# Gated delta net and forgetting attention block: mask and scaling products moved to ScalarE, fp32r low parts from GpSimd to VectorE, output transposes one step later

## The chip, the cores and the metric

The kernel runs on one core of one Trainium2 chip (trn2). The metric is device time in microseconds (us) of one execution, the median of several runs. Engines are named as the profile names them: PE (TensorE matmul), PEld (its weight loads), DVE (VectorE), ACT (ScalarE), POOL (GpSimd), SP (SyncE, which issues most DMAs).

## The reference, cut to what matters

One layer on 1024 tokens of width 1024: input LayerNorm, one input projection, a gated delta net with 4 heads of 128 and forgetting attention with 8 heads of 64, output projection, LayerNorm, squared-ReLU MLP with a gated embedding, LayerNorm. The two parts that the change touches:

```python
# gated delta net, chunks of 64
kk = jnp.einsum('bhnid,bhnjd->bhnij', k, k)
a_mat = jnp.where(strict, kk * beta[..., :, None] * decay, 0.0) + jnp.eye(CHUNK, dtype=f32)
sol = lax.linalg.triangular_solve(a_mat, rhs, left_side=True, lower=True, unit_diagonal=True)
k_dec = k * jnp.exp(gam[..., -1:] - gam)[..., None]
# forgetting attention, blocks of 128 queries
s = s + c_i[..., :, None] - c_all[..., None, :]
attn = jax.nn.softmax(s, axis=-1)
return jnp.einsum('bhqk,bkhd->bqhd', attn.astype(v.dtype), v)
```

## The kernel before, in words

Products in full precision are made of three fp32r matmuls: each operand x is stored as a rounded high part `hi` and a low part `lo = x - hi`, and hi*hi, hi*lo and lo*hi are added up in PSUM. The helper `split_lo(eng, lo, src, hi)` (line 53; its instruction has line L54) makes the low part on the engine that it is given. Another helper, `tt` (L48), is a product, sum or difference of two tensors; `stt` (L51) has a row factor as well. A tile framework orders the instructions of each engine: it follows the program and its priorities, and puts work of low priority where it expects an engine to wait. Each engine then works through its own list in order, and so does each DMA queue.

The stages in order of time: embeddings, LayerNorm and values; the q, k, v columns of the delta net (`conv_silu`, PE tile `g`, three PSUM banks in turn: ACT scales a finished bank into `cv`, DVE adds three shifted products of the bank and takes its last three columns as `edge`, which frees it); then the delta net of heads 0 and 1 (`gdn_a(0)`, `gdn_fs(0)`, `gdn_b(0)`, `gdn_chain(0)`), of heads 2 and 3 (the same with 1), and forgetting attention; after it the output projection (PE tile `ps_mix`), the gate and the MLP, which the change leaves as they are. Projections with low priority (further `g` tiles, then `fq` and `fk` for the attention's q and k, then `gz` for the delta net's gate) fill PE in between.

`gdn_a` computes for each head and each pair of chunks a 128x128 product of keys (PE tile `ps_aq`); DVE scales and masks it into `ka[:, 1]` (line 543, shown as L51). That array goes to DRAM (`img`, lines 549 and 571), from where the 32x32 diagonal blocks come back as `fa`. Lines 550 to 555 multiply `ka[:, 1]` by the mask `m32` into `am` and by `m64` in place, and the keys `kd` by a row factor, six DVE products of 128x1024. `gdn_fs` inverts the diagonal blocks by forward substitution, 62 small DVE instructions (`ftmp`, `ft`), and sends the result through DRAM into `tm` (SP queue) and `ttm` (ACT queue), on which `gdn_b` then works (PE tiles `ps_p`, `ps_tp`, `ps_ttp`).

In attention, `fox_start(h)` loads a head's q and k (`qkr`), casts them to `qa` and `ka` and makes the low parts `qa[64:128]` and `kl`; every second head also loads values (`vr`) and makes `va`. Of the 64 steps (head, block of queries), `fox_a` makes the scores (`ps_sc`), adds the decay with a row minimum on DVE (`s,m`, L758) and takes the exponential on ACT; `fox_b` transposes it (`ps_pt`, two PSUM banks) into `pth` and `ptl`, with POOL writing zeros (`pth<-zero`, `ptl<-zero`); `fox_c` multiplies by the values (`ps_av`), copies that to `ot` on ACT, transposes it (`ps_oq`) and reduces it into `osb`. `fox_pair` normalises a pair of heads (`fsq`, `fss`, `nwt`, `fn`, and a product over `osb`); `fox_out` transposes a pair's outputs into `act_hi` and `act_lo`. `gdn_mix(h)` brings a delta net head into the same arrays: it loads `o` and, from `z_spill`, the gate `szl`, transposes `o` into a bank that it shares with `ps_pt`, and multiplies on DVE. `load_half` loads and splits the output weights (`wo_raw`, `wo`).

In attention POOL makes `ka`, `kl`, the low parts of `va`, of `gdn_mix` and of `wo`, and the last product over `osb`. `o`, `qkr` and `vr` share the two buffers of tag `qk_raw`; `szl` and the `sz` of the gate projection share the three buffers of tag `cv`.

Of the kernel before, what the change touches and what calls it, by code (L numbers as in the profile page):

```python
# [8 lines left out]
F32 = mybir.dt.float32  # L9
# [6 lines left out]
P = 128  # L16
# [6 lines left out]
DH = 64  # L23
# [14 lines left out]
def tile_block(ctx: ExitStack, tc: tile.TileContext, x, p, ln_in_g, ln_in_b, w_in, conv_w, a_log, dt_bias,  # L38
# [432 lines left out]
    nc.vector.memset(m32, 0.0)
    nc.vector.memset(m32[0:32, 32:64], 1.0)
    nc.vector.memset(m32[64:96, 96:128], 1.0)
    nc.vector.memset(m64, 0.0)
    nc.vector.memset(m64[0:64, 64:128], 1.0)
    H = {}

    def gdn_a(hp):
# [68 lines left out]
        for j, h in enumerate(hs):  # L547
            c = H[h]
            nc.sync.dma_start(out=img_full(0, h), in_=c["ka"][:, 1])
            tt(nc.vector, c["am"], c["ka"][:, 1], m32.unsqueeze(1).to_broadcast([P, 8, P]), ALU.mult)  # L550
        for j, h in enumerate(hs):
            c = H[h]
            tt(nc.vector, c["ka"][:, 1], c["ka"][:, 1], m64.unsqueeze(1).to_broadcast([P, 8, P]), ALU.mult)
            tt(nc.vector, c["kd"], c["kd"], cc[:, 1, 8 * j:8 * j + 8].unsqueeze(2).to_broadcast([P, 8, P]), ALU.mult)
        for half in range(2):
# [154 lines left out]
    def fox_load(h):  # L710
        pr, j = h // 2, h % 2
        raw = [fp.tile([P, T], F32, tag="qk_raw", name=f"qkr{h}_{w}", bufs=2) for w in range(2)]
        for w in range(2):
            for half in range(2):
                nc.sync.dma_start(out=raw[w][_sl(half, 64)], in_=qk_spill[w, pr, _sl(j, 64), :])
        qa = fh[j].tile([P, T], F32R, tag="qa", name=f"qa{h}")
        ka = fh[j].tile([P, T], F32R, tag="ka", name=f"ka{h}")
        kl = fh[j].tile([P, T], F32R, tag="kl", name=f"kl{h}")
        nc.scalar.copy(out=qa, in_=raw[0])
        split_lo(nc.vector, qa[64:128], raw[0][64:128], qa[64:128])  # L720
        nc.gpsimd.tensor_copy(out=ka, in_=raw[1])
        split_lo(nc.gpsimd, kl, raw[1], ka)
        cb = fh[j].tile([P, T], F32, tag="cb", name=f"cb{h}")
        nc.sync.dma_start(out=cb, in_=row_spill[32 + h * 8:40 + h * 8, :].rearrange("c i -> (c i)").partition_broadcast(P))
        return qa, ka, kl, cb

    def fox_values(pr):
        raw = fp.tile([P, 8, 2, DH], F32, tag="qk_raw", name=f"vr{pr}", bufs=2)
        nc.sync.dma_start(out=raw.rearrange("q t a d -> q t (a d)"),
                          in_=v_spill[:, _sl(pr)].rearrange("(t q) c -> q t c", q=P))  # L730
        va = []
        for j in range(2):
            va.append(fvp.tile([P, 8, 2, DH], F32R, tag="va", name=f"va{pr}_{j}", bufs=3))
            nc.scalar.copy(out=va[j][:, :, 0], in_=raw[:, :, j])
            split_lo(nc.gpsimd, va[j][:, :, 1], raw[:, :, j], va[j][:, :, 0])
        return va
# [51 lines left out]
    def fox_c(h, g):  # L788

        j = h % 2  # L790
        nk = 2 * g + 2
        va, osb, _ = pairs[h // 2]
        pth, ptl = tiles.pop((h, "c", g))
        po = psf.tile([P, 512], F32, tag="av", name="ps_av", bufs=1)
        for kb in range(nk):
            for i, pt in enumerate((pth, ptl)):
                nc.tensor.matmul(po[:, 0:256], va[j][:, kb].rearrange("q a d -> q (a d)"),  # L797
                                 pt[:, kb].rearrange("q a b -> q (a b)"),
                                 start=(kb == 0 and i == 0), stop=(kb == nk - 1 and i == 1))
        ot = fr.tile([P, 256], F32, tag="ot", name="ot")  # L800
        nc.scalar.copy(out=ot, in_=po[:, 0:256])
        pq = psf.tile([P, 512], F32, tag="av", name="ps_oq", bufs=1)
        for i in range(2):
# [4 lines left out]
    def fox_pair(pr):  # L808
# [14 lines left out]
        tt(nc.vector, fn, fn, lsf, ALU.mult)  # L823
        tt(nc.gpsimd, o16, o16, fn.unsqueeze(2).to_broadcast([P, 16, DH]), ALU.mult)

# [22 lines left out]
    def gdn_mix(h):  # L848
# [3 lines left out]
        for half in range(2):  # L852
            s = cp.tile([P, 512], F32, tag="cv", name="szl", bufs=3)
            nc.sync.dma_start(out=s, in_=z_spill[h, :, _sl(half, 512)])
            ps = psf.tile([P, 512], F32, tag="pt", name="ps_ot")
            for i in range(4):
                nc.tensor.transpose(ps[:, _sl(i)], o[:, half * 4 + i], ident)
            stt(s, ps, gdn_gh, s, ALU.mult, ALU.mult)
            hi = act_hi[half][:, :, h]
            s = s.rearrange("q (t i) -> q t i", i=P)  # L860
            nc.scalar.copy(out=hi, in_=s)
            split_lo(nc.gpsimd, act_lo[half][:, :, h], s, hi)

# [7 lines left out]
    for i in range(n + 12):  # L871
# [63 lines left out]
    def load_half(w, n, tiles, name):  # L935
        out = []
        for k2 in range(NK // 2):
# [534 lines left out]
```

## Time and profile before

| | |
|---|---|
| median of 3 runs | 1447.7 us (1447.67 to 1448.51) |
| the profiled execution, its own time | 1447.75 us |
| its span from first to last instruction | 1446.0 us |
| PE busy | 1387.1 us, 96% |
| DVE busy | 1091.0 us, 75% |
| ACT busy | 553.1 us, 38% |
| POOL busy | 102.6 us, 7% |
| mean granted TensorE clock | 0.992 |

A busy share is a mean over stages. Waits are read from the idle time that a row shows in square brackets, with what ended it; a matmul's own length is longer than the step from its start to the next start, since matmuls are pipelined.

### The profile page before, as it was taken

To read this page: it belongs to the slowest core of one execution; us is meant where nothing else is said; L and a number is where in the kernel's file an instruction comes from. 1 tells how busy PE (TensorE), PEld (TensorE's weight loads), DVE (VectorE), ACT (ScalarE), POOL (GpSimd) and SP (SyncE) were. 2 spreads that over 40 slices of the span, in tenths; PEclk is the share of its full clock that TensorE was granted. 3 is DMA by queue.
4 is the path that set the end of the run, shared out by engine and by line. 5 is a ranking of instruction groups with operands and counts; after the bars stand their busy time and mean duration, and the time that the engine had idled before them with its cause. 6 is when DMAs were issued, how large, how long until landed. Compare 5 with 4: busy or idle time off the path is not lost.

```text
span 1446.0 us, 20592 instructions
## 1 busy us (share of the span) xinstructions
PE 1387.1 (96%) x7342; PEld 1167.7 (81%) x7342; DVE 1091.0 (75%) x2290; ACT 553.1 (38%) x1016; POOL 102.6 (7%) x128
## 2 busy tenths in 40 slices
PE   7999989999999999699999999999999999999997
PEld 5988868988887777578889988888888888888885
DVE  6758899689378886657899776667777689757877
ACT  5223423241247765651124333233333444455421
POOL 1000000000024332440000000000000000000000
PEclk9999999999999999899999999999999999999999
DMA  9856435444553433432476764444444985334342
GB/s 303 252 167 208 124 92 134 130 162 125 146 156 88 124 97 114 131 124 88 153 267 199 214 215 147 139 145 159 155 160 164 310 302 185 96 101 131 110 139 80
DMA packets 195869, 229.10 MB, mean 158 GB/s; under 512 B 23877, under 2 KB 128566, under 8 KB 195766
## 3 DMA queue, kind: packets, MB, share of 16 engines
q1 hardware_dynamic: 186374, 221.48, 48.8%
q10 hardware_dynamic: 9008, 5.24, 1.4%
q8 instruction: 58, 0.95, 0.3%
q0 software_dynamic: 384, 1.06, 0.2%
q14 instruction: 45, 0.37, 0.1%
HBM read 152.14 MB, written 75.60 MB: 157 GB/s over the span
## 4 chain that ended last, share of the span: by engine, by line
PE 78%; DVE 9%; DMA 7%; issue 3%; ACT 2%; POOL 1%; SPq 0%; DVEq 0%; ACTq 0%; POOLq 0%
PE ps_uP L1204 21%; PE ps_da L1324 9%; PE ps_db L1324 9%; PE g L218 6%; PE ps_gP L1071 5%; PE ps_db L1430 3%; PE fk L218 3%; PE ps_mix L950 3%; PE psv L320 3%; PE ps_av L797 2%; PE fq L218 2%; PE gz L218 2%; PE ps_pt L783 2%; DVE h L51 2%; DVE cv L51 1%
## 5 line engine op out<-in xcount | busy, mean ns | idle before, releaser
L1204 PE MATMUL ps_uP<-T,uS 128*128 128x512 f32 x576 | 133.8, 390 | 0.0
L1204 PEld LDWEIGHTS ps_uP<-T,uS 128*128 128x128 f32 x576 | 108.0, 188 | 23.5 <-ACT ua L1209 0.2
L1294 ACT CAST rh<-rr 128x512 fp32r<-128x512 f32 x112 | 69.8, 623 | 141.5 <-PE ps_db L1324 47.9
L54 DVE TENSOR_TENSOR rl<-rr,rh 128x512 fp32r<-128x512 f32 x112 | 77.1, 690 | 57.0 <-ACT rh L1294 28.9
L1204 PE MATMUL ps_uP<-B,uA 128*128 128x512 f32 x384 | 92.2, 395 | 0.0
L950 PE MATMUL ps_mix<-wo,act_hi 128*128 128x512 f32 x256 | 83.0, 399 | 3.5 <-POOL wo L54 1.7
L1204 PEld LDWEIGHTS ps_uP<-B,uA 128*128 128x128 f32 x384 | 72.0, 188 | 17.3
L218 PE MATMUL g<-act_hi,in_hi 128*128 128x512 f32 x192 | 76.4, 398 | 5.0 <-DVE edge L431 5.0
L218 PE MATMUL g<-act_hi,in_lo 128*128 128x512 f32 x192 | 75.9, 397 | 0.6 <-DVE in_lo L54 0.6
L218 PE MATMUL g<-act_lo,in_hi 128*128 128x512 f32 x192 | 75.8, 395 | 0.0
L1294 ACT CAST rl<-B 128x512 fp32r<-128x512 f32 x96 | 59.5, 621 | 22.5 <-PE ps_db L1324 12.4
L54 DVE TENSOR_TENSOR uA<-uraw,uA 128x512 fp32r<-128x512 f32 x48 | 33.2, 692 | 46.0 <-ACT uA L1199 46.0
L1199 ACT CAST uS<-wS 128x512 fp32r<-128x512 f32 x64 | 39.4, 621 | 73.2 <-issue 48.2
L54 DVE TENSOR_TENSOR ql<-B,rl 128x512 fp32r<-128x512 f32 x96 | 65.9, 687 | 0.5 <-ACT rl L1294 0.2
L950 PEld LDWEIGHTS ps_mix<-wo,act_hi 128*128 128x128 f32 x256 | 47.5, 188 | 14.1 <-POOL wo L54 2.4
L783 PE MATMUL ps_pt<-ident,s 128*128 128x128 f32 x288 | 45.3, 277 | 14.1 <-DVE szl L51 8.9
L54 DVE TENSOR_TENSOR ptl<-ps_pt,pth 128x512 fp32r<-128x512 f32 (+2 forms) x96 | 50.9, 552 | 8.0 <-ACT pth L785 7.4
L761 ACT ACTIVATE s<-s,m 128x128 f32<-128x128 f32 (+3 forms) x64 | 50.0, 781 | 14.9 <-DVE m L758 11.4
L51 DVE SCALAR_TENSOR_TENSOR cv<-g,hcw,cv 128x510 f32<-128x510 f32 (+2 forms) x72 | 53.4, 741 | 1.0 <-ACT cv L424 0.5
L1324 PE MATMUL ps_db<-rl,rh 128*128 128x512 f32 x192 | 51.3, 389 | 0.0
L1324 PE MATMUL ps_db<-ql,rh 128*128 128x512 f32 x192 | 51.3, 389 | 0.0
L1324 PE MATMUL ps_db<-rl 128*128 128x512 f32 x192 | 51.3, 389 | 0.0
(369 smaller groups left out, 3675.5 us busy)
## 6 DMA issues: line engine op xcount, KB each, us to landing
uraw<-in_w_up_dram SPq DMA_DIRECT2D x32, 512.0 KB, 4.2
B<-in_w_down_dram SPq DMA_DIRECT2D x32, 512.0 KB, 5.9
rr<-rS SPq DMA_DIRECT2D x64, 256.0 KB, 2.7
in_raw<-in_w_in_dram SPq DMA_DIRECT2D x24, 512.0 KB, 4.3
rr<-rA SPq DMA_DIRECT2D x48, 256.0 KB, 2.9
h_spill<-h SPq DMA_DIRECT2D x16, 512.0 KB, 4.0
qkr<-qk_spill SPq DMA_DIRECT2D x32, 256.0 KB, 4.4
rA<-ub SPq DMA_DIRECT2D x32, 256.0 KB, 2.2
```

What stands on the lines that cost most here:

```text
L51: nc.vector.scalar_tensor_tensor(out=o, in0=a, scalar=s, in1=b, op0=op0, op1=op1)
L54: eng.tensor_tensor(out=lo, in0=src, in1=hi.bitcast(F32), op=ALU.subtract)
L218: mm = nc.tensor.matmul(ps, w[:, k, :], a[n][:, :, k], start=(k == 0 and wi == 0), stop=(k == NK - 1 and wi == 2))
L320: nc.tensor.matmul(ps[:, 0:264], a[t // 4][:, t % 4, k], w[:, k, _sl(n, 264)], start=(k == 0 and wi == 0), stop=(k == NK - 1 and wi == 2))
L761: nc.scalar.activation(out=s[:, :W], in_=s[:, :W], func=AF.Exp, bias=m[:, i:i + 1], scale=-1.0, accum_out=pairs[h // 2][2][:, r, j:j + 1])
L783: nc.tensor.transpose(pt[:, i], s[:, _sl(k0 + i)], ident)
L950: nc.tensor.matmul(ps, a[t // 4][:, t % 4, k], w, start=(k == 0 and wi == 0), stop=(k == NK - 1 and wi == 2))
L1071: nc.tensor.matmul(ps[j // 2][:, j % 2], B[b][s][k][:, _sl(j)], a[w][:, k], start=(first and j % 2 == 0 and k == 0 and wi == 0), stop=(j % ...
L1204: nc.tensor.matmul(ps[p], w[:, k], B[t][b][k], start=(chain is None and k == 0 and wi == 0), stop=(k == 3 and wi == 2), skip_group_check=c ...
L1294: nc.scalar.copy(out=hi, in_=src)
L1324: nc.tensor.matmul(ps[j], rs[x][:, _sl(j)], qs[y], start=(not chain and c == 0 and wi == 0), stop=(c == NP - 1 and wi == 2), skip_group_ch ...
L1430: nc.tensor.matmul(b[j], rs[x][:, i, _sl(j - js[0])], Q[c0 + i][y], start=(c0 == 0 and i == 0 and wi == 0), stop=(c0 + i == NP - 1 and wi ...
```

## The change

In `gdn_a`, the mask products become copies on ACT with a factor per row (0 or 1, from the small table `mrow`) for the column blocks that are kept, and DVE `memset`s for the blocks that are zero; the product on `kd` becomes 16 ACT copies of 128x128 (eight for each head) with the factor of the row. In attention, the cast `ka` goes from POOL to ACT, and the low parts `kl`, `va`, those of `gdn_mix` and of `wo`, and the product over `osb` from POOL to DVE; POOL keeps the zeros. The transposes and the sum of an output block leave `fox_c` and become `fox_d`, one step later. The gate `szl` takes its buffers from tag `th` instead of `cv`.

```diff
-    m32 = gp.tile([P, P], F32, name="m32")
-    m64 = gp.tile([P, P], F32, name="m64")
...
+    mrow = gp.tile([P, 3], F32, name="mrow")
+    nc.vector.memset(mrow, 0.0)
+    for i, (r0, r1) in enumerate(((0, 32), (64, 96), (0, 64))):
+        nc.vector.memset(mrow[r0:r1, i:i + 1], 1.0)
...
             nc.sync.dma_start(out=img_full(0, h), in_=c["ka"][:, 1])
-            tt(nc.vector, c["am"], c["ka"][:, 1], m32.unsqueeze(1).to_broadcast([P, 8, P]), ALU.mult)
+
+            for b0, i in ((32, 0), (96, 1)):
+                nc.scalar.activation(out=c["am"][:, :, b0:b0 + 32], in_=c["ka"][:, 1, :, b0:b0 + 32], func=AF.Copy,
+                                     scale=mrow[:, i:i + 1])
+            nc.vector.memset(c["am"].rearrange("q c (b i) -> q c b i", i=32)[:, :, 0:3:2], 0.0)
         for j, h in enumerate(hs):
             c = H[h]
-            tt(nc.vector, c["ka"][:, 1], c["ka"][:, 1], m64.unsqueeze(1).to_broadcast([P, 8, P]), ALU.mult)
-            tt(nc.vector, c["kd"], c["kd"], cc[:, 1, 8 * j:8 * j + 8].unsqueeze(2).to_broadcast([P, 8, P]), ALU.mult)
+            nc.scalar.activation(out=c["ka"][:, 1, :, 64:128], in_=c["ka"][:, 1, :, 64:128], func=AF.Copy,
+                                 scale=mrow[:, 2:3])
+            nc.vector.memset(c["ka"][:, 1, :, 0:64], 0.0)
+            for ch in range(8):
+                nc.scalar.activation(out=c["kd"][:, ch], in_=c["kd"][:, ch], func=AF.Copy,
+                                     scale=cc[:, 1, 8 * j + ch:8 * j + ch + 1])
...
-        nc.gpsimd.tensor_copy(out=ka, in_=raw[1])
-        split_lo(nc.gpsimd, kl, raw[1], ka)
+        nc.scalar.copy(out=ka, in_=raw[1])
+        split_lo(nc.vector, kl, raw[1], ka)
...
-            split_lo(nc.gpsimd, va[j][:, :, 1], raw[:, :, j], va[j][:, :, 0])
+            split_lo(nc.vector, va[j][:, :, 1], raw[:, :, j], va[j][:, :, 0])
...
-        ot = fr.tile([P, 256], F32, tag="ot", name="ot")
+        ot = tiles[h, "o", g] = fr.tile([P, 256], F32, tag="ot", name="ot")
         nc.scalar.copy(out=ot, in_=po[:, 0:256])
+
+    def fox_d(h, g):
+
+        j, osb, ot = h % 2, pairs[h // 2][1], tiles.pop((h, "o", g))
         pq = psf.tile([P, 512], F32, tag="av", name="ps_oq", bufs=1)
...
-        tt(nc.gpsimd, o16, o16, fn.unsqueeze(2).to_broadcast([P, 16, DH]), ALU.mult)
+        tt(nc.vector, o16, o16, fn.unsqueeze(2).to_broadcast([P, 16, DH]), ALU.mult)
...
-            s = cp.tile([P, 512], F32, tag="cv", name="szl", bufs=3)
+            s = cp.tile([P, 512], F32, tag="th", name="szl", bufs=3)
...
-            split_lo(nc.gpsimd, act_lo[half][:, :, h], s, hi)
+            split_lo(nc.vector, act_lo[half][:, :, h], s, hi)
...
+        if 3 <= i < n + 3:
+            h, r = steps[i - 3]
+            if r % 2:
+                fox_d(h, r // 2)
                 if r == 7 and h % 2:
                     fox_pair(h // 2)
-                    later[max(i + 8, n - 14 + 4 * (h // 2))] = h // 2
+                    later[max(i + 7, n - 14 + 4 * (h // 2))] = h // 2
...
-            split_lo(nc.gpsimd, lo, raw, hi)
+            split_lo(nc.vector, lo, raw, hi)
```

The framework places everything around these edits anew. Three places follow; a number behind a name tells one buffer from another.

First DVE in `gdn_a(0)`, from the first product behind the last `ps_aq` scaling on (`g_1997` and `g_2032` are two projection tiles that follow each other; `vb` are the values). Before:

```order
L48 TENSOR_TENSOR am_1693<-ka_1696,m_1217 128x1024
L48 TENSOR_TENSOR am_1695<-ka_1710,m_1217 128x1024
L48 TENSOR_TENSOR kd_1698<-kd_1698,cc_1794 128x1024
L48 TENSOR_TENSOR ka_1696<-ka_1696,m_1218 128x1024
L48 TENSOR_TENSOR ka_1710<-ka_1710,m_1218 128x1024
L48 TENSOR_TENSOR kd_1712<-kd_1712,cc_1794 128x1024
L48 TENSOR_TENSOR vb_1697<-ps_vt,cc_1794 128x512
...
L48 TENSOR_TENSOR ftmp<-fa_1885,ft_1886 64x31
L51 SCALAR_TENSOR_TENSOR cv<-g_1997,hcw,cv 128x511
...
L431 COPY edge<-g_1997 128x3
```

Now (the tiles are `g_2015` and `g_2050`, and the 511 columns of `g_2015` stand ahead of the `ps_aq` scalings):

```order
L48 TENSOR_TENSOR vb_1695<-ps_vt,cc_1792 128x512
...
L557 MEMSET ka_1694 128x8x64
L51 SCALAR_TENSOR_TENSOR cv<-g_2015,hcw,cv 128x510
L51 SCALAR_TENSOR_TENSOR cv<-g_2050,hcw,cv 128x511
L557 MEMSET ka_1708 128x8x64
L51 SCALAR_TENSOR_TENSOR cv<-g_2015,hcw,cv 128x509
L431 COPY edge<-g_2015 128x3
...
L48 TENSOR_TENSOR ftmp<-fa_1903,ft_1904 64x31
```

Six products left the list, two memsets entered it, and `edge` now stands ahead of the forward substitution instead of behind its first steps.

Second DVE at the end of `gdn_fs(0)`; `fa<-ft` is the copy behind its last step. Before, with `g_2348` the last but two of the `g` tiles (`g_2392` and `g_2427` follow):

```order
L48 TENSOR_TENSOR ftmp<-fa_1885,ft_1886 64x31
L51 SCALAR_TENSOR_TENSOR cv<-th,cv 128x512
L48 TENSOR_TENSOR ft_1886<-ft_1886,ftmp 64x31
L51 SCALAR_TENSOR_TENSOR cv<-g_2348,hcw,cv 128x511
L579 COPY fa_1885<-ft_1886 64x1024
```

Now, with `g_2445` the very last of them:

```order
L48 TENSOR_TENSOR ftmp<-fa_1903,ft_1904 64x31
L51 SCALAR_TENSOR_TENSOR cv<-g_2445,hcw,cv 128x511
L48 TENSOR_TENSOR ft_1904<-ft_1904,ftmp 64x31
L51 SCALAR_TENSOR_TENSOR cv<-edge,hcw,cv 128x1
L585 COPY fa_1903<-ft_1904 64x1024
```

The last step of the substitution moved from ahead of the products on `g_2348` to behind the first product on the last `g` tile. On PE, 24 `fq` matmuls stand between that last `g` tile and the first `ps_p` before, and 47 now.

Third the SP queue in heads 6 and 7 of the attention (`o`, `qkr` and `szl` as above). Before:

```order
L851 DMA o_6021<-o_spill 128x1024
L458 DMA z_spill<-sz 128x512
L724 DMA cb_6090<-row_spill 128x1024
L715 DMA qkr_0_6077<-qk_spill 64x1024 x2
L940 DMA wo_raw<-in_w_out_dram 128x2x512
L715 DMA qkr_1_6078<-qk_spill 64x1024 x2
L458 DMA z_spill<-sz 128x512 x2
L851 DMA o_6248<-o_spill 128x1024
L854 DMA szl<-z_spill 128x512 x2
```

Now:

```order
L861 DMA o_6059<-o_spill 128x1024
L458 DMA z_spill<-sz 128x512
L730 DMA cb_6124<-row_spill 128x1024
L721 DMA qkr_0_6111<-qk_spill 64x1024 x2
L864 DMA szl<-z_spill 128x512 x2
L721 DMA qkr_1_6112<-qk_spill 64x1024 x2
L864 DMA szl<-z_spill 128x512 x2
L954 DMA wo_raw<-in_w_out_dram 128x2x512
L861 DMA o_6286<-o_spill 128x1024
```

Before, the first `szl` stands behind the third `o` (`o_6248`); now three `szl` have gone out still earlier, among the loads of the first heads, and the next four stand ahead of that `o` (`o_6286`).

## Rows read from the trace of the kernel before

**Rows 1.** The page's chain that ended last: shares of the span by engine.

```profile
PE 78%; DVE 9%; DMA 7%; issue 3%; ACT 2%; POOL 1%; SPq 0%; DVEq 0%; ACTq 0%; POOLq 0%
```

**Rows 2.** Windows: stretch, its length, each engine's busy us and count, granted clock, DMA share, GB/s.

```profile
420.00:650.00 230.00, 208.13 (x1286) 169.52 (x1285) 168.53 (x449) 142.59 (x322) 91.61 (x106) 0.98 0.39 117
506.50:529.00 22.50, 21.39 (x143) 17.73 (x142) 19.58 (x57) 16.44 (x39) 6.51 (x10) 1.00 0.30 84
578.00:600.00 22.00, 12.42 (x65) 9.31 (x66) 11.02 (x27) 10.72 (x24) 10.87 (x9) 0.77 0.54 168
```

**Rows 3.** Timeline of DVE, 176 to 202 us: start, us, what; in brackets idle before.

```profile
183.34 2.35 DVE L48 TENSOR_TENSOR am<-ka,m 128x1024 f32<-128x1024 f32 x2
...
187.77 1.23 DVE L48 TENSOR_TENSOR ka<-ka,m 128x1024 f32<-128x1024 f32 x1 [0.94 <-DMA img<-ka]
...
190.40 1.22 DVE L48 TENSOR_TENSOR kd<-kd,cc 128x1024 f32<-128x1024 f32 x1
...
195.58 0.73 DVE L51 SCALAR_TENSOR_TENSOR cv<-g,hcw,cv 128x510 f32<-128x510 f32 x1
...
197.18 0.15 DVE L431 COPY edge<-g 128x3 f32<-128x3 f32 x1
```

**Rows 4.** Timeline of PE, 196 to 203 us.

```profile
197.48 0.77 PE L218 MATMUL g<-act_hi,in_hi 128*128 128x512 f32 x1 [4.96 <-DVE edge L431]
...
202.15 0.39 PE L218 MATMUL g<-act_hi,in_lo 128*128 128x512 f32 x1
```

**Rows 5.** The chain in order of time: start, us, what.

```profile
113.93 48.54 PE g L218 x214
```

**Rows 6.** Timeline of ACT, 186 to 188.5 us.

```profile
186.89 1.05 ACT L190 CAST in_hi<-in_raw 128x1024 fp32r<-128x1024 f32 x1 [8.95 <-PE g L218]
```

**Rows 7.** Timelines of DVE and of ACT's queue, 241 to 262 us.

```profile
241.90 0.18 DVE L48 TENSOR_TENSOR ft<-ft,ftmp 64x31 f32<-64x31 f32 x1
...
249.11 1.04 ACTq L583 DMA_DIRECT2D ttm<-img  x2
```

**Rows 8.** DMA issues, 241 to 262 us: count, KB each, median us to landing.

```profile
ttm<-img ACTq DMA_DIRECT2D x2, 512.0 KB, 7.7
```

**Rows 9.** Timelines of POOL, DVE and PE, 440 to 452 us.

```profile
445.25 2.40 POOL L54 TENSOR_TENSOR kl<-qkr,ka 128x1024 fp32r<-128x1024 f32 x1
...
445.97 2.77 DVE L54 TENSOR_TENSOR qa<-qkr,qa 64x1024 fp32r<-64x1024 f32 x1
...
449.52 1.12 PE L783 MATMUL ps_pt<-ident,s 128*128 128x128 f32 x8 [1.05 <-DVE ptl L54]
```

**Rows 10.** Timelines of POOL, SP and PE, 570 to 592 us.

```profile
578.69 2.34 POOL L54 TENSOR_TENSOR kl<-qkr,ka 128x1024 fp32r<-128x1024 f32 x1
...
581.05 0.32 SPq L851 DMA_DIRECT2D o<-o_spill  x1
581.47 0.86 SPq L854 DMA_DIRECT2D szl<-z_spill  x2
...
586.88 0.45 PE L783 MATMUL ps_pt<-ident,s 128*128 128x128 f32 x1 [8.92 <-DVE szl L51]
```

**Rows 11.** Groups by line and shape, DVE, 420 to 650 us: count, busy us, mean ns, idle before.

```profile
L54 DVE TENSOR_TENSOR qa<-qkr,qa 64x1024 fp32r<-64x1024 f32 x6 | 13.9, 2321 | 0.2
...
L48 DVE TENSOR_TENSOR nwt<-fn 128x16 f32<-128x16 f32 x12 | 4.2, 347 | 0.2
L51 DVE SCALAR_TENSOR_TENSOR fn<-nwt,fn 128x16 f32<-128x16 f32 x12 | 3.8, 320 | 0.2
L54 DVE TENSOR_TENSOR in_lo<-in_raw,in_hi 128x1024 fp32r<-128x1024 f32 x3 | 3.7, 1225 | 2.3 <-ACT in_hi L190 2.3
```

**Rows 12.** The same of ACT, 160 to 440 us.

```profile
L652 ACT ACTIVATE vb<-ps_o,rr 128x128 f32<-128x128 f32 x32 | 10.0, 364 | 33.6 <-PE ps_o L651 33.5
```

**Rows 13.** Timelines of POOL and DVE at 530 us.

```profile
530.31 0.36 POOL L776 CAST pth<-zero 128x128 fp32r<-128x128 f32 x1 [6.14 <-PE ps_av L797]
...
530.34 0.17 DVE L51 SCALAR_TENSOR_TENSOR fn<-nwt,fn 128x16 f32<-128x16 f32 x1
```

More of the change, by code (lines that the diff above doesn't have):

```diff
@@ L468, in tile_block @@
     psx = pxs.enter_context(tc.tile_pool(name="psg", bufs=5, space=PS, reuse_waits="tile"))
-    m32 = gp.tile([P, P], F32, name="m32")
-    m64 = gp.tile([P, P], F32, name="m64")
[L471 to L475, printed above, removed]
+    mrow = gp.tile([P, 3], F32, name="mrow")
+    nc.vector.memset(mrow, 0.0)
+    for i, (r0, r1) in enumerate(((0, 32), (64, 96), (0, 64))):
+        nc.vector.memset(mrow[r0:r1, i:i + 1], 1.0)
     H = {}
@@ L791, in fox_c @@
         nk = 2 * g + 2
-        va, osb, _ = pairs[h // 2]
+        va = pairs[h // 2][0]
         pth, ptl = tiles.pop((h, "c", g))
```

## The prediction

> **What bounds the kernel now.** I read the chain of waits first: it runs through PE for 78% of the span, DVE is next with 9% [rows 1]. PE's matmuls are a fixed amount of work, so a change can win only where PE stands idle or runs at a low clock, and only in the stages that it touches: `gdn_a` to `gdn_chain` (some 160 to 420 us) and attention (420 to 650 us). PE's own timeline and a table of windows then show where it waits there.
>
> In `gdn_a(0)` PE waits 4.96 us for DVE's `edge`, which frees a bank [rows 4]. DVE is late because, from 183.34 to the end of the product that starts at 190.40, it makes the six mask and key products, with a wait for the transfer of `img` among them, and only then comes to the projection's products, so that `edge` is made at 197.18 [rows 3]. Behind the wait PE is slow: 11 matmuls begin from 197.48 to 202.15 [rows 4], 4.67 us, against 2.50 us at the usual step of 48.54/214 = 0.227 us [rows 5]. So the place costs about 5.0 + 2.2 = 7.2 us.
>
> In attention PE is busy for 208.1 of 230 us [rows 2]. The idle time has two kinds. In heads 1 to 5, PE waits about a microsecond for DVE's `ptl`; the row shown is followed back to `qa`, which took DVE 2.77 us while POOL made `kl` [rows 9], though a product with twice the rows and as many columns (`in_lo`) takes 1.225 us [rows 11]. And at 586.88 PE has waited 8.92 us for `szl`: POOL's `kl` holds a `qk_raw` buffer until 581.03, SP issues `o` into it at 581.05, and `szl`, next in SP's list, goes out at 581.47 [rows 10]. The mean clock of the 22 us there is 0.77 [rows 2]; I count 2 us for it, as in `gdn_a(0)`.
>
> **The change, part by part.**
>
> *Masks and keys.* Six DVE products go: 2.35 us for two, and four like 1.22 or 1.23 [rows 3], 7.2 us of DVE. The memsets that replace them clear less than half as much and have no such row; I take 0.3 us each, an estimate at a quarter of a product (bounds 0 and 1.22). The first still waits for `img`, as the product at 187.77 did [rows 3]. Then four products on `g` and the second memset stand ahead of `edge` (first order excerpt): 187.8 + 2 x 0.3 + 3 x 0.73 [rows 3] gives about 190.6, and about 1.6 us more because the first product on the bank now stands ahead of the `ps_aq` scalings, where ScalarE's copy of the bank must come first. That is 192.2; PE wants the bank at 197.48 - 4.96 = 192.5. The wait goes, and the slow matmuls with it: -7.2 us.
>
> ACT gets 16 + 6 copies for each pair of heads. A copy of 128x128 with a row factor took 0.364 us [rows 12], so `kd` costs at most 5.8 us. They lie in the 8.95 us in which ACT waited for PE before 186.89 [rows 6], so I cost them at nothing; without that cover they would delay a cast by some 2 us, with two further banks between it and PE.
>
> *What is late next in the delta net.* The second excerpt ties the end of the substitution to the last `g` tile. After PE ends that tile, one DVE product (0.73 [rows 3]), an ACT copy of the same bank ahead of it, for which I take the same, and the step itself later, some 1.7 us, the substitution ends. Before, from the start of its last step at 241.90 to the issue of `ttm` at 249.11 [rows 7] and its landing 7.7 us later [rows 8], 14.9 us passed, mostly transfers. So `ttm` lands about 16.5 us behind the last `g` tile. PE has 47 `fq` matmuls of 0.227, 10.7 us, before the first `ps_p`, and then eight `ps_p` of a quarter of the columns and three more of the projections, between 0.7 us (the three alone) and 2.5 us (all eleven at 0.227); I take the middle, 1.6. So it waits 16.5 - 12.3 = 4.2 us, a new wait in place of the old. The delta net wins 7.2 - 4.2 = 3 us (bounds 0 and 7.2). In `gdn_a(1)` the substitution starts with the landing of `fa`, as before, and I leave its place on PE as it was: nothing.
>
> *Attention: DVE's balance.* DVE takes over, in the stretch, six `kl`, four products over `osb` and eight `wo`, each 128x1024 at 1.225 us [rows 11], which is 22.0 us, and eight `va` and eight low parts in `gdn_mix` at half the size, 0.61 us, 9.8 us. It gets back what POOL's products cost it: six `qa` at 2.321 instead of 1.225 us, twelve `nwt` at 0.347 and twelve `fn` at 0.320 [rows 11] instead of the 0.17 that `fn` takes undisturbed [rows 13]: 6.6 + 2.1 + 1.8 = 10.5 us. So DVE's 168.5 us [rows 2] become 168.5 + 31.8 - 10.5 = 189.8 us. ACT gains six `ka` of about 1 us and has 142.6 of 230 us busy [rows 2]; nothing.
>
> *Attention: PE.* Its floor is its 208.1 us less the 2 us of slow clock, 206 us. The upper end comes from DVE: in the head of 506.5 to 529 us it was busy for 19.58 of 22.5 us, 87% [rows 2], and 189.8/0.87 = 218 us. PE and DVE will both be nearly full, and in-order lists lose something at such a balance; neither row is nearer, so I take the middle, 212 us: -18 us (bounds -24 and -12). The stall at 586.88 goes, since `szl` now stands ahead of the `o` that held it (third excerpt) and its buffers no longer wait for the gate projection; so do the waits behind `qa`.
>
> *The rest.* `fox_d` one step later takes PE's `ps_oq` away from right behind ACT's `ot`; its work is the same, and behind the last head over 45 `ps_mix` matmuls cover the later product on `osb`: nothing.
>
> *A rule against the change.* POOL keeps its zeros, which read SBUF, beside 34 more DVE products of two SBUF operands. The rows show one such product, `fn`, start 0.03 us into a `pth<-zero` of 0.36 us and take 0.17 us [rows 13], as without one. The Trainium skill, SBUF — State Buffer, Who interferes with whom, says that a DVE instruction with two SBUF inputs contends with a GpSimd instruction that reads SBUF, and that whichever starts first blocks the other. The trace agrees where POOL has a product and not where it has this copy, so the sum stays.
>
> *Sum.* 1447.75 us (the profiled execution's own time, span 1446.0; the median is 1447.7, the same) - 3 - 18 = 1426.75: **1427 us**.
>
> **The rivals.**
>
> 1. *SP still holds `szl` back*, because a new entry ahead of it waits for a buffer (`qkr` for `o`'s, or `szl` itself for a `th` buffer). For: SP is one list and 10 transfers share two buffers. Against: three `szl` go out long before. Price: 8.9 + 2 of attention's gain stay lost, 1427 + 11 = **1438 us**.
> 2. *The delta net wins nothing*, since the wait for `ttm` eats the whole 7.2 us. For: transfers are long [rows 8]. Against: 47 `fq` cover most. 1427 + 3 = **1430 us**.
> 3. *The zeros block DVE*, each pair of them one product. Some 28 pairs stand in the stretch; at 2 x 0.36 us [rows 13], 20 us for DVE: (189.8 + 20)/0.9, with 0.9 the density of my forecast (189.8/212), is 233 us, so attention wins nothing: 1447.75 - 3 + 3 = **1448 us**. Against: the `fn` above [rows 13]. By the Trainium skill (SBUF — State Buffer, Who interferes with whom) this is what would come.
> 4. *Slower: DVE's list becomes the bound.* Its moved products stand in order ahead of the row minima, and each waits for an ACT cast or a transfer; everything in attention then waits. The density of the whole stretch was 168.5/230 = 73%. If it does not rise, 189.8/0.73 = 260 us, +30 us, less 3: **1475 us**. It decides where the density stays under 189.8/233 = 81%. For: POOL's work was off the path and DVE's is on it. Against: DVE idled before mostly because PE or POOL held it, and one head already ran at 87% [rows 2].
> 5. *The fast end*: PE loses nothing in either place, 1447.75 - 7 - 24 = **1417 us**.
>
> **How the numbers follow.** Forecast (1420 to 1434) 0.60, rival 1 0.12, rival 2 0.08, rival 3 0.06, rival 4 0.07, rival 5 0.07. The range that holds eight in ten takes in the forecast, rivals 1, 2 and 5: 1416 to 1439 us, with rivals 3 and 4 outside. A measurement of this kernel can tell about 0.2%, 2.9 us. Faster by more than that (below 1444.8): 0.60 + 0.12 + 0.08 + 0.07 and a little of rivals 3 and 4, 0.89. Within it, most of rival 3: 0.05. Slower, most of rival 4: 0.06.
>
> **What the profile of the changed kernel would show.** PE without the wait for `edge` near 192 us; a wait of some 4 us for a transfer at the first `ps_tp`; `qa` at about 1.2 us; no wait of PE for `szl`; attention some 18 us shorter with DVE busy for about 90% of it. I am wrong if `ps_pt` or `ps_sc` waits for DVE in most heads for a microsecond or more (rival 4), if `nwt` or `kl` on DVE still show lengths of 2 us beside the zeros (rival 3), or if SP's `szl` again follows a long wait (rival 1).

## The result, and the profile after

| | before | changed |
|---|---|---|
| median | 1448.11 us (1447.67 to 1449.73) | 1428.93 us (1428.83 to 1430.14) |
| span of the profiled execution | 1446.0 us | 1427.2 us |
| PE busy | 1387.1 us, 96% | 1381.9 us, 97% |
| DVE busy | 1091.0 us, 75% | 1095.0 us, 77% |
| POOL busy | 102.6 us | 31.2 us |

The ratio to the kernel before is 0.9867 with a 95% interval of 0.985 to 0.9885: 19 us faster, where 21 were forecast (1427 us, range 1416 to 1439).

Where the 19 us came from is read best at equal work. For each trace I added up PE's matmuls in the order of their starts, each counted at the usual step from one start to the next of its shape. The table gives the time at which PE has done as much as the kernel before had done at the time in the first column, as the difference to it (us; negative is earlier). The columns from `x1_masks` on are single-part kernels that come below.

| before at | place | changed | x1_masks | x2_att | x3_szl | x4_moves | x7_fk0 |
|---|---|---|---|---|---|---|---|
| 158.9 | ahead of `gdn_a(0)` | 0.0 | 0.8 | 0.8 | 1.3 | -0.7 | -0.1 |
| 251.9 | ahead of `gdn_b(0)` | -9.3 | -8.3 | 0.7 | 1.3 | -1.0 | -9.3 |
| 272.5 | `gdn_b(0)` nearly done | -2.1 | -1.3 | 0.7 | 1.8 | -1.4 | -8.0 |
| 446.1 | attention has begun | -1.8 | -2.3 | -0.6 | 0.6 | -3.1 | -6.3 |
| 591.3 | behind the old wait for `szl` | -22.3 | -3.9 | -19.3 | -5.9 | -15.7 | -19.4 |
| 662.8 | attention is over | -18.7 | -0.5 | -20.6 | -7.3 | -15.6 | -15.5 |

So the delta net won 9.3 us and handed 7.2 of them back within 20 us; attention won about 17 us net, and had won more before its last heads (at the 22.3 us the changed kernel's PE is at 569 us, ahead of the two waits of heads 6 and 7 that are shown below).

DVE around the old wait, in the changed kernel's timeline (columns as in [rows 3]): the two memsets take 0.48 us each, and `edge` is made at 190.34 instead of 197.18 us [rows 3].

```profile
187.65 0.48 DVE L557 MEMSET ka<- 128x512 f32 x1 [0.87 <-DMA img<-ka]
...
189.39 0.48 DVE L557 MEMSET ka<- 128x512 f32 x1
189.79 0.62 DVE L51 SCALAR_TENSOR_TENSOR cv<-g,hcw,cv 128x509 f32<-128x509 f32 x1
190.34 0.15 DVE L431 COPY edge<-g 128x3 f32<-128x3 f32 x1
```

PE has no wait there any more [rows 4]. What it has instead, in its timeline at `gdn_b(0)`, is two waits for `tm`:

```profile
254.44 1.16 PE L603 MATMUL ps_p<-tm,am 128*128 128x128 f32 x8 [3.02 <-DMA tm<-img]
258.88 1.26 PE L603 MATMUL ps_p<-tm,am 128*128 128x128 f32 x8 [2.58 <-DMA tm<-img]
259.94 1.92 PE L612 MATMUL ps_tp<-pm,ttm 128*128 128x128 f32 x8
```

The DMA issues, before (241 to 262 us) and then now (240 to 262 us), show these transfers taking longer. Now the landing of one `tm` and one `ttm` is recorded, 7.7 and 11.2 us after the issue; before, the same two took 5.2 and 8.6 us (the medians shown are of two issues each).

```profile
tm<-img SPq DMA_DIRECT2D x2, 512.0 KB, 5.8
```

```profile
in_raw<-in_w_in_dram SPq DMA_DIRECT2D x2, 512.0 KB, 5.2
tm<-img SPq DMA_DIRECT2D x2, 512.0 KB, 7.7
ttm<-img ACTq DMA_DIRECT2D x2, 512.0 KB, 11.2
```

Projection weights, `qk_spill` and `conv_spill` move in that stretch in both kernels (5.00 MB in all before, 4.72 now). What differs in SP's list is that a load of projection weights goes out 0.47 us ahead of `tm`, where it was 5.6 us; whether that lengthens the transfers was not tried.

The windows of the changed kernel (columns as in [rows 2]). Attention's work, which filled 420 to 650 us before, now ends 19 us sooner; in 420 to 631 us DVE is busy for 183.80 us, 87%. In the 8 us from 258 on, behind PE's two waits, the clock is 0.79, a mean of the two levels of 1.2 and 2.4 GHz, and in heads 6 and 7 there is a stretch in which DVE is busy for 19.51 of 20 us and PE for 15.37.

```profile
420.00:631.00 211.00, 202.60 (x1290) 169.69 (x1290) 183.80 (x482) 150.29 (x333) 24.40 (x64) 0.98 0.41 123
258.00:266.00 8.00, 7.12 (x49) 7.15 (x50) 2.75 (x4) 0.58 (x1) 0.00 (x0) 0.79 0.38 116
```

```profile
560.00:580.00 20.00, 15.37 (x102) 12.51 (x101) 19.51 (x53) 14.21 (x32) 1.48 (x4) 0.93 0.50 139
580.00:600.00 20.00, 17.50 (x109) 15.27 (x110) 17.56 (x39) 13.97 (x28) 2.65 (x6) 0.81 0.33 112
```

DVE's groups by line and shape in 420 to 650 us (columns as in [rows 11]): `qa` takes 1222 ns instead of 2321, `fn` 183 instead of 320, `nwt` 168 instead of 347.

```profile
L54 DVE TENSOR_TENSOR kl<-qkr,ka 128x1024 fp32r<-128x1024 f32 x7 | 8.5, 1221 | 0.6 <-ACT ka L727 0.6
L54 DVE TENSOR_TENSOR qa<-qkr,qa 64x1024 fp32r<-64x1024 f32 x6 | 7.3, 1222 | 0.2
L51 DVE SCALAR_TENSOR_TENSOR fn<-nwt,fn 128x16 f32<-128x16 f32 x12 | 2.2, 183 | 0.1
L48 DVE TENSOR_TENSOR nwt<-fn 128x16 f32<-128x16 f32 x12 | 2.0, 168 | 0.2
```

The waits of a microsecond of PE for `ptl` in heads 1 to 5 [rows 9] and the wait for `szl` [rows 10] are gone. Two long ones are left in heads 6 and 7, in PE's timeline:

```profile
579.92 0.88 PE L789 MATMUL ps_pt<-ident,s 128*128 128x128 f32 x3 [3.94 <-DVE fn L51]
591.51 0.69 PE L814 MATMUL ps_oq<-ident,ot 128*128 128x128 f32 x2 [2.32 <-ACT ot L807]
```

DVE's timeline ahead of the first shows what holds it. The releaser named is `fn`, but the product that empties the bank is `ptl` at 579.09 us; ahead of it stand `wo`, `qa` and `kl`, three products of 1.22 us, one behind the other:

```profile
575.19 1.22 DVE L54 TENSOR_TENSOR wo<-wo_raw,wo 128x1024 fp32r<-128x1024 f32 x1
...
576.53 1.22 DVE L54 TENSOR_TENSOR qa<-qkr,qa 64x1024 fp32r<-64x1024 f32 x1
...
577.87 1.22 DVE L54 TENSOR_TENSOR kl<-qkr,ka 128x1024 fp32r<-128x1024 f32 x1
...
579.09 0.68 DVE L54 TENSOR_TENSOR ptl<-ps_pt,pth 128x512 fp32r<-128x512 f32 x1
```

The second is not DVE's. It ends with `ot`, and ahead of that ACT's timeline is full from 585.98 us on, with two exponentials, two casts of output weights, an `act_hi` and a `pth`:

```profile
587.01 1.98 ACT L956 CAST wo<-wo_raw 128x1024 fp32r<-128x1024 f32 x2
...
591.07 0.38 ACT L807 COPY ot<-ps_av 128x256 f32<-128x256 f32 x1
```

### The profile page after: what moved, and what is told of

Its sections match the earlier page's. It is cut to its first block, busy times and chain, and to the rows that moved or that the text cites. A ratio compares the mean times of both kernels' runs of the same rounds, so it can differ in the third digit from the quotient of the medians.

```text
span 1427.2 us, 20603 instructions
## 1 busy us (share of the span) xinstructions
PE 1381.9 (97%) x7342; PEld 1170.9 (82%) x7342; DVE 1095.0 (77%) x2321; ACT 577.4 (40%) x1068; POOL 31.2 (2%) x84
## 4 chain that ended last, share of the span: by engine, by line
PE 50%; DVE 4%; DMA 2%; issue 1%; SPq 0%; ACT 0%; DVEq 0%; ACTq 0%
PE ps_uP L1218 22%; PE ps_da L1338 9%; PE ps_db L1338 9%; PE ps_gP L1085 4%; PE ps_db L1444 3%; PE ps_mix L964 2%; DVE h L51 1%; DMA r<-t_spill 1%; DVE st L140 1%; DMA h<-h_spill 1%; DMA h_spill<-h 0%; PE ps_tr L971 0%; DMA wo_raw<-in_w_out_dram 0%; DMA hb<-h_spill 0%; DVE t L48 0%
## 5 line engine op out<-in xcount | busy, mean ns | idle before, releaser
L791 ACT CAST pth<-ps_pt 128x512 fp32r<-128x512 f32 (+2 forms) x96 | 43.8, 482 | 24.9 <-PE ps_pt L789 23.9
L51 DVE SCALAR_TENSOR_TENSOR cv<-g,hcw,cv 128x511 f32<-128x511 f32 (+2 forms) x72 | 52.9, 736 | 1.1 <-ACT cv L424 0.7
L1338 PE MATMUL ps_da<-rl 128*128 128x512 f32 x192 | 51.3, 389 | 0.0
```

The lines of the kernel that those rows point to most:

```text
L51: nc.vector.scalar_tensor_tensor(out=o, in0=a, scalar=s, in1=b, op0=op0, op1=op1)
L791: nc.scalar.copy(out=hi, in_=pt[:, :kn])
L1338: nc.tensor.matmul(ps[j], rs[x][:, _sl(j)], qs[y], start=(not chain and c == 0 and wi == 0), stop=(c == NP - 1 and wi == 2), skip_group_ch ...
```

## Experiments: the parts one by one

Twelve kernels were run. Every ratio is to the kernel before on the same chip, with its 95% interval.

**`x1_masks`: the delta net's part alone.** Edit to the kernel before: the hunks of `gdn_a` of the change (with `mrow` in place of `m32` and `m64`), nothing else.

> The kernel before with the edit of gdn_a alone (mask and key products to ScalarE copies, DVE memsets). Theory (what it wins at `edge` comes back as a wait for `tm` and `ttm` at the first ps_p and ps_tp): PE reaches the end of the g tiles 9 us sooner, then waits some 6 us and runs slowly for another microsecond: 1446 to 1447 us against 1448. Rival (the delta net's win passes on, and attention gave back the rest): 1439 to 1441 us.

Measured 0.9992 (0.9979 to 1.0006), 1445.55 us against 1447.11: no difference that can be measured. The table shows 8.3 us won ahead of `gdn_b(0)` and 1.3 left behind it. PE's timeline has the same two waits as the changed kernel:

```profile
254.77 1.16 PE L602 MATMUL ps_p<-tm,am 128*128 128x128 f32 x8 [2.35 <-DMA tm<-img]
259.76 2.05 PE L602 MATMUL ps_p<-tm,am 128*128 128x128 f32 x8 [2.78 <-DMA tm<-img]
```

So the theory holds: the win is real where it was looked for, and comes back at the next transfer.

How much comes back differs from trace to trace. Six of the kernels below have the `gdn_a` of the changed kernel. Between the same two rows of the table, 251.9 and 272.5, they hand back 4.4 us (`x5_nofoxd`), 4.1 (`x6_klpool`), 4.9 (`x8_wopool`), 5.3 (`x9_zeros`), 7.1 (`x10_quart`) and 7.1 (`x11_quart3`), where the changed kernel hands back 7.2. Their two waits for `tm` add up to between 2.9 and 5.6 us. The clock is 0.79 behind the second wait (258 to 266 us) in the changed kernel and the last two, 0.79 in the 8 us before that in `x6_klpool` and `x9_zeros`, and 1.00 in both stretches in the other two. So 7.2 us is the figure of one trace, at the upper end.

**`x2_att`: the attention part alone.** Edit to the changed kernel: `gdn_a` and its masks as before.

> The changed kernel with gdn_a as before, so the attention edits alone. Theory (attention wins by itself, independent of the delta net): 1448 - 17 = 1431 us, PE's wait of 5 us for `edge` back, DVE some 195 us busy in the 230 us of attention. Rival (the two parts help each other, since projections left over from the delta net fill attention's gaps): 1435 us or more.

Measured 0.9868 (0.985 to 0.9886), 1427.23 us: the whole gain of the change, without the masks, and 4 us below the theory's 1431. PE's wait for `edge` is back:

```profile
197.87 0.77 PE L218 MATMUL g<-act_hi,in_hi 128*128 128x512 f32 x1 [5.15 <-DVE edge L431]
```

With `x1_masks` this says that the delta net's part adds nothing that can be measured, and that attention does not need it.

**`x3_szl`: the gate's buffers alone.**

```diff
-            s = cp.tile([P, 512], F32, tag="cv", name="szl", bufs=3)
+            s = cp.tile([P, 512], F32, tag="th", name="szl", bufs=3)
```

> The kernel before with szl's buffers taken from tag th and nothing else. Theory (SP's list, with szl behind an `o` that waits for POOL, is what makes the wait of 8.9 us, and its place alone cures it): 1437 us. Rival (POOL's `kl` is what is late; with szl out early, PE waits at the same place for the next thing that POOL makes, or for the `szl` that still stand behind `o`): 1443 to 1447 us.

Measured 0.9956 (0.9944 to 0.9969), 1440.11 us: between the two. The wait for `szl` is gone, and two smaller ones stand close by, the second for a low part that POOL makes:

```profile
578.34 0.66 PE L857 MATMUL ps_ot<-ident,o 128*128 128x128 f32 x4 [1.15 <-DVE act_lo L51]
583.71 0.50 PE L950 MATMUL ps_mix<-wo,act_lo 128*128 128x512 f32 x1 [2.26 <-POOL act_lo L54]
```

So one line of the change takes about 6 us, and the rest of that stall needs POOL's work to be elsewhere.

**`x4_moves`: the moves off POOL alone.** Edit to the kernel before: `ka` to ScalarE; `kl`, `va`, the low parts of `gdn_mix` and `wo`, and the product over `osb` to DVE; nothing on `szl` or `fox_d`.

> The kernel before with the moves from POOL to DVE and ACT alone (ka, kl, va, gdn_mix, wo, osb); szl stays in tag cv, fox_d isn't there. Theory (POOL's products held both DVE and the buffer that SP waits for): qa at 1.22 us, the waits of a microsecond per head gone, the wait for szl down to 3 us or less: 1434 to 1438 us. Rival (DVE's list becomes the bound): 1445 us or more, with ps_pt waiting for DVE in most heads.

Measured 0.9905 (0.9891 to 0.9919), 1433.17 us: the theory, a microsecond below its range, and the largest part of the gain. By the table it is 12.6 us further ahead at 591 us than at 446, and it keeps a wait for `szl`, shorter than the 8.92 us of [rows 10] but longer than I expected:

```profile
571.14 0.45 PE L783 MATMUL ps_pt<-ident,s 128*128 128x128 f32 x1 [4.75 <-DVE szl L51]
```

**`x5_nofoxd`: without the later transposes.** Edit to the changed kernel: the transposes and the sum of `fox_d` back at the end of `fox_c`.

> The changed kernel with the transposes and the sum of fox_d back in fox_c. Theory (that step is worth nothing): the changed kernel's time, 1428 us, within 3. Rival (PE's waits for ACT's `ot` come back, 32 places at a tenth of a microsecond and some at 1.3): 1432 to 1436 us.

Measured 0.9902 (0.9889 to 0.9915), 1433.12 us: slower than the changed kernel by some 5 us. My theory (worth nothing) falls by its number, but the rival's reason does not show either: waits of PE for `ot` do not come back. In heads 6 and 7 its waits are for row minima and `ptl` (0.8 to 1.4 us), and one for the output weights at 625 us:

```profile
589.56 0.38 PE L759 MATMUL ps_sc<-ka,qa 128*128 128x256 f32 x1 [1.43 <-DVE m L764]
...
625.15 1.22 PE L956 MATMUL ps_mix<-wo,act_hi 128*128 128x512 f32 x2 [2.28 <-ACT wo L948]
```

The order of DVE's and ScalarE's lists in the last heads is another one. By the table's measure this trace is 3.6 us ahead of the changed kernel's at 446 us, since it hands back less at `gdn_b(0)`, and 3.6 us behind at 663: it loses 7 us to it in attention. Why the later step gives the better order was not tried.

**`x6_klpool`: keys back on POOL.**

```diff
-        nc.scalar.copy(out=ka, in_=raw[1])
-        split_lo(nc.vector, kl, raw[1], ka)
+        nc.gpsimd.tensor_copy(out=ka, in_=raw[1])
+        split_lo(nc.gpsimd, kl, raw[1], ka)
```

> The changed kernel with `ka` and `kl` back on POOL, all else as changed. Theory (POOL's product with two SBUF operands holds DVE's): qa back at some 2.3 us, PE waits of about 1.2 us in most heads again: 1434 to 1437 us. Rival (the gain of attention is SP's order of szl alone, and the products' engine does not matter): 1428 us, within 3.

Measured 0.9924 (0.9909 to 0.994), 1435.45 us: 8 us are lost again, as the theory said. The timelines of POOL and then of DVE at 486 us show the hold at its plainest. Two DVE instructions of 16 columns, which take 0.17 us in the changed kernel, take as long as what POOL is doing: 1.04 us beside the cast `ka`, and 1.91 us until `kl` ends.

```profile
486.07 1.04 POOL L727 CAST ka<-qkr 128x1024 fp32r<-128x1024 f32 x1 [0.72 <-PE ps_sc L759]
487.19 2.35 POOL L54 TENSOR_TENSOR kl<-qkr,ka 128x1024 fp32r<-128x1024 f32 x1
```

```profile
486.10 1.04 DVE L48 TENSOR_TENSOR nwt<-fn 128x16 f32<-128x16 f32 x1
487.06 0.68 DVE L54 TENSOR_TENSOR ptl<-ps_pt,pth 128x512 fp32r<-128x512 f32 x1
487.66 1.91 DVE L51 SCALAR_TENSOR_TENSOR nwt<-nwt,fss 128x16 f32<-128x16 f32 x1
```

The `ptl` between them reads one of its operands from PSUM. In this row it is not held: it takes its usual 0.68 us, most of that while POOL is in `kl`, and `kl` is no longer than usual either.

**`x8_wopool`: the weights' low parts back on POOL.** Edit to the changed kernel: `split_lo(nc.vector, lo, raw, hi)` in `load_half` with `nc.gpsimd`.

> The changed kernel with the low parts of `wo` back on POOL, all else as changed. Theory (DVE is what PE waits for in heads 6 and 7, and a POOL product of two SBUF operands holds DVE's for longer than DVE would need for it): no gain, 1428 to 1433 us. Rival (these eight products were off the path on POOL, and moving them to DVE cost what PE waits for at 575 to 592 us): 1421 to 1425 us.

Measured 0.991 (0.9894 to 0.9926), 1435.08 us: 6 us slower than the changed kernel, and 2 above the theory's range. The rival falls, and the hold that the theory names is there. At 575 us POOL's `wo` takes 2.37 us, and beside it a DVE `nwt` of 16 columns takes 1.87 us:

```profile
575.72 1.87 DVE L51 SCALAR_TENSOR_TENSOR nwt<-nwt,fss 128x16 f32<-128x16 f32 x1
```

But PE's `ps_mix` also waits for POOL's `wo` itself, 3.0 us in three places. How the 6 us divide between the hold and the slower product is not shown.

**`x9_zeros`: POOL's zeros four times.**

```diff
-            nc.gpsimd.tensor_copy(out=pth[:, nk - 1, 0], in_=zero)
-            nc.gpsimd.tensor_copy(out=ptl[:, nk - 1, 0], in_=zero)
+            for _ in range(4):
+                nc.gpsimd.tensor_copy(out=pth[:, nk - 1, 0], in_=zero)
+                nc.gpsimd.tensor_copy(out=ptl[:, nk - 1, 0], in_=zero)
```

> The changed kernel with each of POOL's two zero casts written four times, so some 190 more casts of 0.29 us, 55 us of POOL. Theory (a POOL cast of one SBUF operand does not hold DVE's products; POOL waits instead): the changed kernel's time, 1428 us, within 3, with fn, nwt, qa and kl at the lengths that they have now. Rival (it holds them, as POOL's products did): DVE's products with two SBUF operands grow to 1.5 us and more, 1440 us or more.

Measured 0.9868 (0.9856 to 0.9881), 1428.0 us: the changed kernel's time, with POOL's zero casts at 85 us instead of 26. The groups of POOL and of DVE in 420 to 650 us:

```profile
L783 POOL CAST pth<-zero 128x128 fp32r<-128x128 f32 x128 | 44.3, 346 | 290.8 <-PE ps_o L657 174.2 <-PE ps_av L804 93.8 <-DVE ptl L54 17.7
L784 POOL CAST ptl<-zero 128x128 fp32r<-128x128 f32 x128 | 41.2, 322 | 0.4
```

```profile
L54 DVE TENSOR_TENSOR qa<-qkr,qa 64x1024 fp32r<-64x1024 f32 x6 | 7.4, 1233 | 0.2
L51 DVE SCALAR_TENSOR_TENSOR fn<-nwt,fn 128x16 f32<-128x16 f32 x12 | 2.2, 187 | 0.1
```

`qa` grew from 1222 to 1233 ns, `fn` from 183 to 187. So the zeros cost nothing; what that says of the mechanism comes in the last section.

## Experiments: attempts at more

**`x7_fk0`: cover for the wait at `gdn_b(0)`.**

```diff
-    with tc.issue_after(last_mm["fq0", 0]):
+    with tc.issue_after(last_mm["fk0", 0]):
```

> The changed kernel with gdn_b(0) kept back until the first half of fk0 instead of fq0: 24 more projection matmuls (5.4 us) ahead of the first ps_p. Theory (what the delta net lost is a wait for tm and ttm that more matmuls would cover): the wait of 6 us and the slow clock behind it go, 1422 to 1424 us. Rival (the projections are only borrowed; with fewer of them left PE waits later, in gdn_chain or gdn_b(1)): 1427 to 1430 us.

Measured 0.9881 (0.9867 to 0.9896), 1430.3 us: no gain over the changed kernel. The first half of the theory holds: the waits at `gdn_b(0)` shrink from 3.02 and 2.58 us to this,

```profile
258.57 1.13 PE L603 MATMUL ps_p<-tm,am 128*128 128x128 f32 x8 [0.58 <-DMA tm<-img]
260.51 1.16 PE L612 MATMUL ps_tp<-pm,ttm 128*128 128x128 f32 x8 [0.82 <-ACT pm L605]
```

and PE comes into attention 6.3 us ahead of the kernel before, 4.5 ahead of the changed one. The lead is lost in attention, by 591 us, and turned round in heads 6 and 7, where it ends 3 us behind the changed kernel. The rival's number holds, but neither theory named that place. The 4.5 us are no more than traces without this line differ by: `x5_nofoxd` and `x6_klpool` come into attention 5.4 and 6.4 us ahead of the kernel before.

**`x10_quart`, `x11_quart3`, `x12_fk0q`: smaller pieces for DVE.** `x10_quart` splits each `wo` low part by columns:

```diff
-            split_lo(nc.vector, lo, raw, hi)
+            for q in range(4):
+                split_lo(nc.vector, lo.rearrange("q k c -> q (k c)")[:, _sl(q, 256)], raw.rearrange("q k c -> q (k c)")[:, _sl(q, 256)],
+                         hi.rearrange("q k c -> q (k c)")[:, _sl(q, 256)])
```

`x11_quart3` does the same to `qa` and `kl` as well, and `x12_fk0q` adds the line of `x7_fk0`.

> The changed kernel with each `wo` low part made in four pieces of 256 columns, so that `ptl` and the row minima can stand between them. Theory (PE's waits of 4.1 and 2.4 us in heads 6 and 7 come from two or three products of 1.22 us in a row on DVE): 1422 to 1426 us. Rival (DVE is full there, 19.5 of 20 us, so the order of its list changes nothing): 1428 us, within 3.

> As the run before, with `qa` and `kl` in four pieces each as well. Theory: another 1 to 3 us, 1420 to 1425 us. Rival (DVE is full; the fixed part of 48 more instructions, some 0.06 us each, is added to it): 1428 to 1432 us.

> As the run before, with gdn_b(0) behind the first half of fk0 too, which won 6 us up to 330 us and 4.5 us up to 440 us and lost it again in heads 6 and 7. Theory (the loss there was DVE's order, which the pieces cure): 1417 to 1423 us. Rival (heads 6 and 7 have a time of their own, set by DVE's work, and take back what comes early): the same as the run before, within 2.

Measured 0.9899 (0.9885 to 0.9913), 0.9895 (0.988 to 0.991) and 0.9885 (0.9867 to 0.9904): no gain from any. By their ratios the first two are some 4 us slower than the changed kernel, but their intervals touch or overlap its 0.985 to 0.9885. The pieces do not help, as the framework does not put `ptl` between them; PE's wait for it, 3.94 us in the changed kernel, is 5.46 us in `x10_quart` (the row below) and 6.59 us in `x12_fk0q`:

```profile
583.30 0.87 PE L789 MATMUL ps_pt<-ident,s 128*128 128x128 f32 x3 [5.46 <-DVE ptl L54]
```

In DVE's timeline of `x10_quart` four pieces, `qa`, `kl` and now the product over `osb` stand ahead of `ptl`:

```profile
577.05 0.42 DVE L54 TENSOR_TENSOR wo<-wo_raw,wo 128x256 fp32r<-128x256 f32 x1
...
578.85 1.22 DVE L54 TENSOR_TENSOR qa<-qkr,qa 64x1024 fp32r<-64x1024 f32 x1
...
580.20 1.22 DVE L54 TENSOR_TENSOR kl<-qkr,ka 128x1024 fp32r<-128x1024 f32 x1
581.33 1.22 DVE L48 TENSOR_TENSOR osb<-osb,fn 128x1024 f32<-128x1024 f32 x1
582.47 1.02 DVE L54 TENSOR_TENSOR ptl<-ps_pt,pth 128x512 fp32r<-128x512 f32 x2
```

So heads 6 and 7 take back what comes early, as the rival of `x12_fk0q` said: by the table's measure that kernel is 5.3 us ahead at 446 us, where the changed one is 1.8 ahead, and 16.6 against 18.7 at 663. The load of the last head, the output weights and the gate meet there on DVE, and on ACT too. An order that puts `ptl` ahead of these products by hand was not tried. No kernel measured beats the changed one; `x2_att` and `x9_zeros` equal it.

## Why the prediction was right

The time, 1428.93 us, lies 2 us from the forecast. By the table the delta net won 1.8 us where 3 were forecast, and attention 16.9 where 18 were. That it came so close is in part luck, as the point on `fox_d` shows. Step by step:

- **The wait for `edge` goes, -7.2 us.** Right: -9.3 us by the table, 8.5 of them by 211 us (the same sum, at a row that the table leaves out). `edge` came at 190.34 us, where I had 192.2: three products on `g`, not the four that I wrote, and the memsets stood ahead of it, and the 1.6 us that I added for the bank's first product were not there. The memsets clear half of the array, not less, and took 0.48 us, inside the bounds of 0 and 1.22 and above the 0.3 taken.
- **A new wait, +4.2 us.** Right in kind and place, too small for this trace: 3.02 + 2.58 = 5.6 us of waiting, and by the table 9.3 - 2.1 = 7.2 us in all, the upper bound that I gave; the six other traces lie between 4.1 and 7.1. PE waits at `ps_p` for `tm`, and I had counted those `ps_p` as work that covers a wait for `ttm` at `ps_tp`. The mis-sized term is "`ttm` lands about 16.5 us behind the last `g` tile". I took the transfers as long as before; the second `ttm` took 11.2 us instead of 8.6 and could first be used at 259.94 us, 19.3 us behind the end of that tile at about 240.6. And I counted slow matmuls behind the old wait but not behind the new one, where the clock is 0.79 for 8 us. Rival 2 (the delta net wins nothing) is what `x1_masks` measured within its interval, though 2 us stay in the table.
- **DVE in attention, 189.8 us busy at a density between 87% and nearly full.** Measured 183.80 us in 211 us, 87%: 6 us less busy time than I costed, at the density of the one head that I had read [rows 2]. None of the costed products is short: the lengths of DVE's instructions add up to 193.0 us in 420 to 650 us before and to 213.6 in 420 to 631 now, 20.6 more, where I had 31.8 - 10.5 = 21.3. My error was to add lengths to busy time, which counts a moment in which two records overlap only once, and which grew by 15.3 us. The stage's length, 212 us in the forecast, is 230 - 16.9 = 213 by the table: the error in the busy time and the one in the density, 189.8/212 or 90%, cancel.
- **POOL's hold on DVE, 10.5 us given back.** Right: `qa`, `nwt` and `fn` are at 1222, 168 and 183 ns, and `x6_klpool` and `x8_wopool` show 8 and 6 us when POOL gets a part of the work again (in `x8_wopool` not through the hold alone).
- **The wait for `szl`, 9 to 11 us.** Right that it goes, so rival 1 did not come. The place in SP's list is worth 6 us by itself (`x3_szl`), and the moves alone leave a wait of 4.75 us for `szl` (`x4_moves`): both SP's order and the moves off POOL were needed.
- **"`fox_d` one step later: nothing."** Wrong. Without it the kernel is 5 us slower (`x5_nofoxd`). Its own work was costed rightly as the same; what I left out is that moving it gives the framework another order for the last heads; why that order is better stays open. What I did cost came to about 1433 us (`x5_nofoxd`), 6 above the forecast, and the 5 us that I put at nothing closed most of the gap.
- **Rival 4, DVE's list becomes the bound.** It did not decide, as 87% lies above its 81%. But it holds in one place of heads 6 and 7, the wait of 3.94 us; the other, of 2.32 us, is ACT's. With these two and a mean clock of 0.81 in 580 to 600 us PE's lead falls from 22.3 to 18.7 us.
- **Rival 3, the zeros.** Right in the sum, by `x9_zeros`; the reason that I read from the trace was too simple (below).

## What to carry to other kernels

A stall that ends with a buffer coming free is worth what the next wait leaves of it: follow the freed engine to its next transfer, and size that transfer with what else will be moving then. When work goes from a second engine to the nearly full one, count what the second engine's products had held up; here 32 us of new DVE work still won time, since 10 us of holds went and PE's waits behind them with them. Add lengths to lengths, and not to busy time. And where an in-order list is full for 20 us, a lead won earlier can be lost there (`x7_fk0`, `x12_fk0q`), so look at that stretch first.

## What the runs showed of the chip

**POOL's casts hold DVE too, for their own length, and DVE holds them.** I had read from `fn` [rows 13] that a POOL cast of one SBUF operand does not hold a DVE product. `x6_klpool` shows that it does: `nwt` took 1.04 us beside the cast `ka` of 1.04 us. The trace of the kernel before has it too, in a row that the prediction does not use: a `nwt` that starts 0.34 us into the `ka` cast of 487.13 us takes 0.73 us and ends with the cast. In [rows 13] it is the cast that is longer than its usual 0.29 us, at 0.36; with starts 0.03 us apart, that row does not show which came first. The Trainium skill, SBUF — State Buffer, Who interferes with whom, has a DVE instruction with two SBUF inputs contend with any GpSimd instruction that reads SBUF, and whichever is issued first hold the other. These traces agree.

The zeros are cheap for another reason. They last 0.29 us, so there is little that one can hold DVE for, and in 14 of the 20 overlaps with such DVE instructions in the changed kernel's attention DVE was there first; in the other six the DVE instruction is at most 0.1 us longer than usual. In the changed kernel a zero cast takes 1.25 us beside a DVE product of 1.22 that began 0.13 us sooner (POOL's row, then DVE's):

```profile
457.65 1.25 POOL L782 CAST pth<-zero 128x128 fp32r<-128x128 f32 x1 [6.41 <-DVE sz L51]
```

```profile
457.52 1.22 DVE L54 TENSOR_TENSOR in_lo<-in_raw,in_hi 128x1024 fp32r<-128x1024 f32 x1
```

Where `x9_zeros` has eight casts in a row, DVE's small instructions start 0.24 us apart, the same as POOL's casts, and take 0.20 us each (POOL's rows, then DVE's). Behind the last cast, from the third DVE row on, they take 0.17 us and start 0.21 us apart, so the price is 0.03 us for each.

```profile
424.39 0.29 POOL L783 CAST pth<-zero 128x128 fp32r<-128x128 f32 x1
424.62 0.29 POOL L784 CAST ptl<-zero 128x128 fp32r<-128x128 f32 x1
```

```profile
424.50 0.20 DVE L48 TENSOR_TENSOR nwt<-ro 128x16 f32<-128x16 f32 x1
424.74 0.20 DVE L51 SCALAR_TENSOR_TENSOR nwt<-nwt,sso 128x16 f32<-128x16 f32 x1
...
425.93 0.17 DVE L48 TENSOR_TENSOR nwt<-ro 128x16 f32<-128x16 f32 x1
```
